# An attention layer's output stage: all five engines in program order, each block's operands joined two blocks ahead

## The chip, the cores and the metric

The kernel runs on one core of a Trainium2 chip. The metric is the device time of one execution in microseconds (us). Engines: PE (TensorE, matmuls; its weight loads are a row of their own, PEld), DVE (VectorE), ACT (ScalarE), POOL (GpSimd), and SP (SyncE), whose queue (SPq) issues all the transfers that this text speaks of. PEclk is the granted TensorE clock, where 1.00 is the 2.4 GHz level and 0.50 the 1.2 GHz level.

## The reference, cut to what matters

Two sequences, a prompt of 1024 tokens and a sample of 2048, go through the same layer. The last lines are what the change is about; the two attentions in front of them are cut to their results.

```python
def hybrid_layer(x, c, w_in, w_out, w_ada, b_ada, ln_g, ln_b, ...):
    shift, scale, gate = jnp.split(jax.nn.silu(c) @ w_ada + b_ada, 3, axis=-1)
    proj = (x * (1.0 + scale[:, None]) + shift[:, None]) @ w_in
    qa, ka, va, ga, qb, kb, vb, gb = jnp.split(proj, SPLIT_OFFSETS, axis=-1)
    oa = window_gqa(qa, ka, va, sink, rel_bias) * jax.nn.silu(ga)
    ob = diff_attention(qb, kb, vb, ...) * jax.nn.silu(gb)     # softmax 1 - lam * softmax 2, then rms_norm
    h = jnp.concatenate([oa, ob], axis=-1) @ w_out             # 1024 x 1024
    return layer_norm(ALPHA * x + gate[:, None] * h, ln_g, ln_b)
```

Every product is wanted at float32's precision. The kernel gets it by splitting each operand into a high part (rounded to the format that PE multiplies at full rate) and a low part (the rest), and multiplying three times: high by high, high by low, low by high.

## The kernel before, in words

The kernel projects, runs the windowed attention (its gated result goes to DRAM as `OA`), and then the differential attention, as a pipeline of *units* (a head and a stretch of queries). A call `slot(n, ...)` does four steps j = 0..3; in each it makes a part of the logits of unit n, the transposes of an earlier unit, and the value products of one still earlier. The unnormalised result of a head goes to DRAM as `OT` (line 876), the row of norm factors as `frow` (line 894); the gate silu(gb) has been in DRAM as `GB` for long.

When the logits of the last unit are issued (unit N-1), six more slots (24 steps) drain the transposes and values. Into each of these steps the kernel puts one step of a generator, `outputs()`, which is printed at the end of this section and does the output product `h` and the layer norm in 24 blocks of 128 tokens: 16 of the sample, then 8 of the prompt. Its parts are:

- `stage` loads w_out; `split_weights(k)` splits 128 rows of it: DVE scales rows 4 to 7 (L989), ACT makes the high half (L990), DVE and POOL the low halves (L991).
- `load_rest(t)` issues five transfers on SP's queue for block t: OT (L999, 256 KB), frow broadcast to all partitions (L1000, 256 KB in SBUF), GB (L1001, 256 KB), OA (L1002, 256 KB), and x (L1004, 512 KB). There are four buffers for the first four (`dat`) and six for x (`xts`).
- `join(t)` makes the left operand of block t: POOL multiplies OT by frow (L1012) and by GB (L1013); then for each of two halves ACT rounds it to the high part (L1016) and POOL subtracts for the low part (L1017). Half 0 is OA and needs only its transfer; half 1 is the product of L1013. There are three buffers for the result (`os_`).
- `output(B)` runs 48 matmuls 128x128 by 128x512 for a block (L1042, L1043, L1044: 2 column halves x 8 k x 3 products) into PSUM (four banks `po`, two to a block), and yields 15 times among them. Behind them stands the layer norm: DVE L1047, L1048, L1051, L1055, L1057; POOL L1058 (the power -1/2); DVE L1080; ACT L1082 twice (from PSUM into x's buffer); POOL L1083 twice (adds the norm's bias); SP L1084 stores 512 KB. The last block has a finer form of its own.

**What sets the order.** In the manual stretch each named engine gets its instructions in the order in which the program writes them. Before, this holds for PE, SP and POOL; ACT's and DVE's order in the tail is made by the framework's scheduler. In the program, `load_rest(t + 3)` comes at step 2 of block t's output and so, on SP, behind the store of block t-1; `join(t + 1)` comes at step 4 of block t's output, and so, on POOL, ahead of the norm of block t (L1058, L1083). Every engine's queue is worked off strictly in its order: an instruction that waits holds up all behind it. A transfer on SP's queue also waits for the one eight transfers before it.

Of the kernel before, what the change touches and what calls it, by code (L numbers as in the profile page):

```python
# [15 lines left out]
PSUM = bass.MemoryType.PSUM  # L16
DRAM = bass.MemoryType.DRAM

PE, SP, POOL = mybir.EngineType.PE, mybir.EngineType.SP, mybir.EngineType.Pool
P = 128  # L20
D = 1024
KC = D // P
# [44 lines left out]
def hybrid_layer(ctx, tc, x_prompt, x_sample, c_prompt, c_sample, w_in, w_out, w_ada, b_ada, ln_g, ln_b,  # L67
# [829 lines left out]
    def slot(n, extra, other=None):  # L897
        for j in range(4):
            if extra:
                fill(extra)  # L900
            if n < N:
                logits(n, j)
                prefetch(n, j)
            for g, piece in values_at.get(n, ()):
                if piece % 4 == j:
                    values(g, piece)
            if 0 <= n - LAG < N:
                transpose(n - LAG, j)
            if j == 1 and n in sums_at:
                square_sum(sums_at[n])  # L910
            if other is not None:
                next(other, None)
# [59 lines left out]
    def stage(ks):  # L972
        for k in ks:
            raws[k] = early_p.tile([P, D], F32, tag="wo", name="raw") if k < 4 else row_halves()
            nc.sync.dma_start(out=raws[k], in_=w_out[k * P:(k + 1) * P, :])
# [7 lines left out]
    def split_weights(k):  # L983
        woH[k], woL[k] = wmem[2 * k](), wmem[2 * k + 1]()
        raw = raws.pop(k)
        for n in range(2):
            ns = slice(n * 512, (n + 1) * 512)
            if k >= 4:
                nc.vector.tensor_scalar(out=raw[:, ns], in0=raw[:, ns], scalar1=wsub, scalar2=None, op0=ALU.mult)  # L989
            nc.scalar.copy(woH[k][:, ns], raw[:, ns])  # L990
            (nc.vector if n else nc.gpsimd).tensor_tensor(  # L991
                out=woL[k][:, ns], in0=raw[:, ns], in1=woH[k][:, ns].bitcast(F32), op=ALU.subtract)

    def load_rest(t):

        s, i = order[t]
        cs = slice(i * P, (i + 1) * P)
        d = dat.next().rearrange("p (n i q) -> p n i q", n=4, i=4)
        nc.sync.dma_start(out=d[:, 1], in_=OT[s][:, :, cs].rearrange("k r t -> r k t"))  # L999
        nc.sync.dma_start(out=d[:, 2], in_=frow[s][:, cs].partition_broadcast(P))  # L1000
        nc.sync.dma_start(out=d[:, 3], in_=GB[s][:, :, cs].rearrange("k r t -> r k t"))  # L1001
        nc.sync.dma_start(out=d[:, 0], in_=OA[s][:, :, cs].rearrange("i r t -> r i t"))  # L1002
        xt = xts.next().bitcast(F32)
        nc.sync.dma_start(out=xt, in_=xs[s][cs, :])  # L1004
        Bs[t] = dict(s=s, i=i, d=d, xt=xt)

    def join(t):

        B = Bs[t]
        d = B["d"]  # L1010
        B["oH"], B["oL"] = [v.rearrange("p (k q) -> p k q", k=KC) for v in os_.next()]
        nc.gpsimd.tensor_tensor(out=d[:, 1], in0=d[:, 1], in1=d[:, 2], op=ALU.mult)  # L1012
        nc.gpsimd.tensor_tensor(out=d[:, 1], in0=d[:, 1], in1=d[:, 3], op=ALU.mult)  # L1013
        for half in range(2):
            hs = slice(half * 4, half * 4 + 4)
            nc.scalar.copy(B["oH"][:, hs, :], d[:, half])  # L1016
            nc.gpsimd.tensor_tensor(out=B["oL"][:, hs, :], in0=d[:, half], in1=B["oH"][:, hs, :].bitcast(F32),  # L1017
                                    op=ALU.subtract)


    def load_gate(s):
        keep[s] = part().bitcast(F32)
        nc.sync.dma_start(out=keep[s], in_=grow[s, :].partition_broadcast(P))

    def load_norm():
        for name, v in (("g", ln_g), ("b", ln_b)):
            keep[name] = part().bitcast(F32)
            nc.sync.dma_start(out=keep[name], in_=v.partition_broadcast(P))
# [58 lines left out]
    NB = len(order)  # L1087
    Bs = {}

    def outputs():  # L1090

        stage((4, 5, 6, 7))
        load_rest(0)
        yield
        for k in range(4):
            split_weights(k)
            yield
        load_gate(1)
        yield
        yield  # L1100
        load_norm()
        yield
        for k in range(4, KC):
            split_weights(k)
            if k == 5:
                join(0)
                load_rest(1)
            yield
        load_rest(2)
        for t in range(NB):  # L1110
            if t == 8:
                load_gate(0)
            for j, _ in enumerate(output(Bs[t], t == NB - 1)):
                if j == 2 and t + 3 < NB:
                    load_rest(t + 3)
                if j == 4 and t + 1 < NB:
                    join(t + 1)
                yield
            del Bs[t]
            yield  # L1120
# [5 lines left out]
    lst.close()  # L1126
    ps_po = pool(st, "ps_po", 4, PSUM)
    other = outputs()
    with tc.manual_schedule(engines={PE, SP, POOL}):
        for n in range(N, max(sums_at) + 1):  # L1130
            slot(n, 0, other)
        for _ in other:
            pass
# [27 lines left out]
```

## Time and profile before

| | us |
|---|---|
| median of 3 runs | 2265.22 (2263.21, 2265.22, 2272.9) |
| the profiled execution, its own time | 2257.25 |
| its span from first to last instruction | 2255.5 |
| what lies around the span | 1.75 |
| PE busy | 2099.9 (93%) |
| DVE, POOL, ACT busy | 1296.5 (57%), 1154.6 (51%), 1037.2 (46%) |

The profiled execution is 7.97 us under the median of the runs. The stretch that the change touches begins at about 1800 us. The views read here are the table of windows (busy time of each engine between two moments), the timeline (every instruction of an engine with its start, its time and, in square brackets, the idle time before it with what ended it), the chain of waits, and the table of waits.

### The profile page before, as it was taken

How to read it: one execution, taken by the hardware profiler on the slowest of the kernel's cores; microseconds unless marked ns; L12 is line 12 of the kernel's file. 1: busy time of each engine (PE TensorE's matmuls, PEld its weight loads, DVE VectorE, ACT ScalarE, POOL GpSimd, SP SyncE). 2: the span in 40 equal slices, each digit the busy share in tenths (PEclk: the TensorE clock that was granted, in tenths of full speed). 3: DMA queues.
4: the chain of work that ended last, by engine and by line, in shares of the span. 5: the costliest groups of instructions: out<-in, count | busy, mean ns of one | idle time of the engine just before them, and what ended most of it. 6: DMA issues, size and time to landing. Idle time of an engine off the chain costs nothing.

```text
span 2255.5 us, 32659 instructions
## 1 busy us (share of the span) xinstructions
PE 2099.9 (93%) x11597; PEld 1793.1 (80%) x11597; DVE 1296.5 (57%) x2538; ACT 1037.2 (46%) x2022; POOL 1154.6 (51%) x836
## 2 busy tenths in 40 slices
PE   7999999999999999999999999999999966777787
PEld 4777988888988788888879999999998854555666
DVE  5343224212246676666459999999998942333444
ACT  5211113111136677666347777777788841111111
POOL 3223223222243343333449888989888952454554
PEclk9999999999999999999999999999999977988999
DMA  8676536445368678775341332314136676454552
GB/s 271 179 261 184 150 126 181 133 118 150 117 186 227 171 190 214 203 192 157 118 151 36 98 63 77 83 39 114 45 91 134 102 99 121 113 137 117 145 150 95
DMA packets 340203, 312.46 MB, mean 139 GB/s; under 512 B 32086, under 2 KB 296950, under 8 KB 339656
## 3 DMA queue, kind: packets, MB, share of 16 engines
q1 hardware_dynamic: 340040, 310.37, 52.1%
q8 instruction: 92, 1.51, 0.4%
q14 instruction: 71, 0.58, 0.2%
HBM read 212.70 MB, written 97.60 MB: 138 GB/s over the span
## 4 chain that ended last, share of the span: by engine, by line
PE 70%; DMA 16%; SPq 4%; DVE 3%; POOL 3%; issue 2%; ACT 1%; ACTq 0%; DVEq 0%; POOLq 0%
PE lg L814 12%; PE pj L186 11%; PE pj L187 11%; PE pj L188 11%; DMA l<-oa 8%; PE tp L852 5%; PE ac L872 3%; PE ac L871 3%; PE ac L870 3%; PE lgA L607 3%; PE tp L643 2%; DMA Q<-qb 2%; PE ac L635 2%; POOL vt L1083 1%; PE ac L634 1%
## 5 line engine op out<-in xcount | busy, mean ns | idle before, releaser
L186 PE MATMUL pj<-uH,wH 128*128 128x512 f32 x1040 | 417.4, 401 | 5.1 <-DVE gg L257 5.1
L188 PE MATMUL pj<-uH,wL 128*128 128x512 f32 x1040 | 407.5, 392 | 0.0
L187 PE MATMUL pj<-uL,wH 128*128 128x512 f32 x1040 | 407.0, 391 | 0.0
L217 POOL TENSOR_TENSOR wL<-wr,wH 128x1024 fp32r<-128x1024 f32 x74 | 181.9, 2460 | 410.7 <-DVE wH L215 368.2
L814 PE MATMUL lg<-kt,Q 128*128 128x512 f32 x1280 | 377.2, 416 | 8.3 <-DMA Q<-qb 6.1
L838 POOL TENSOR_TENSOR l<-l,l 128x1024 f32<-128x1024 f32 x160 | 382.8, 2413 | 0.9
L827 ACT ACTIVATE l<-l,nm 128x2048 f32<-128x2048 f32 (+1 forms) x192 | 331.0, 1724 | 20.9 <-DVE nm L819 20.9
L814 PEld LDWEIGHTS lg<-kt,Q 128*128 128x128 f32 x1280 | 217.3, 190 | 40.8 <-issue 6.6
L819 DVE CUSTOM_DVE_ANT_0 l<-lg,W 128x1024 f32<-128x1024 f32 x192 | 233.2, 1215 | 18.0 <-PE lg L814 17.6
L836 POOL TENSOR_SCALAR l<-l,s 128x1024 f32<-128x1024 f32 x160 | 179.8, 1135 | 116.1 <-DVE s L832 51.2
L854 ACT CAST pth<-tp 128x512 fp32r<-128x512 f32 x320 | 186.2, 583 | 113.6 <-PE tp L852 109.4
L188 PEld LDWEIGHTS pj<-uH,wL 128*128 128x128 f32 x1040 | 195.4, 188 | 42.4
L186 PEld LDWEIGHTS pj<-uH,wH 128*128 128x128 f32 x1040 | 195.9, 188 | 36.8 <-DVE gg L257 5.9
L187 PEld LDWEIGHTS pj<-uL,wH 128*128 128x128 f32 x1040 | 196.2, 189 | 29.9
L855 DVE TENSOR_TENSOR ptl<-tp,pth 128x512 fp32r<-128x512 f32 x320 | 208.7, 684 | 12.1 <-ACT pth L854 10.8
L852 PE MATMUL tp<-ident,l 128*128 128x128 f32 x1280 | 195.9, 276 | 17.1 <-DVE ptl L855 17.0
L872 PE MATMUL ac<-pth,vt 128*128 128x256 f32 x640 | 183.4, 287 | 0.0
L870 PE MATMUL ac<-pth,vt 128*128 128x256 f32 x640 | 183.0, 286 | 0.0
L871 PE MATMUL ac<-ptl,vt 128*128 128x256 f32 x640 | 182.7, 285 | 0.0
L622 POOL TENSOR_SCALAR l<-l,rcA 128x384 f32<-128x384 f32 (+1 forms) x144 | 81.5, 585 | 196.2 <-PE ac L634 85.1
L819 DVE CUSTOM_DVE_ANT_0 l<-lg,W,nm 128x1024 f32<-128x1024 f32 x128 | 164.0, 1281 | 23.7 <-PE lg L814 16.5
L852 PEld LDWEIGHTS tp<-ident,l 128*128 128x128 f32 x1280 | 150.9, 143 | 19.9 <-DVE ptl L855 9.1
(209 smaller groups left out, 4069.8 us busy)
## 6 DMA issues: line engine op xcount, KB each, us to landing
wr<-in_w_in SPq DMA_DIRECT2D x39, 1024.0 KB, 5.4
KAt<-ka SPq DMA_DIRECT2D x40, 384.0 KB, 9.6
QAt<-qa SPq DMA_DIRECT2D x24, 512.0 KB, 4.0
kt<-kb SPq DMA_DIRECT2D x24, 512.0 KB, 9.1
Q<-qb SPq DMA_DIRECT2D x48, 256.0 KB, 3.0
Q<-qb SPq DMA_DIRECT2D x96, 128.0 KB, 4.4
vt<-vb SPq DMA_DIRECT2D x48, 256.0 KB, 5.6
out<-vt SPq DMA_DIRECT2D x20, 512.0 KB, 3.1
```

The costliest lines, as they stand in the source:

```text
L186: nc.tensor.matmul(acc, lhsT=a(k), rhs=b(k), start=(k == 0), stop=False)
L187: nc.tensor.matmul(acc, lhsT=a(k), rhs=bl(k), start=False, stop=False)
L188: nc.tensor.matmul(acc, lhsT=al(k), rhs=b(k), start=False, stop=(k == KC - 1))
L814: nc.tensor.matmul(L[:, c * CH:(c + 1) * CH], lhsT=G["Q"][:, v, m, b * P:(b + 1) * P], rhs=Kt[kt0 + c][:, m, :], start=(v == 0), stop=(v = ...
L819: nc.vector.tensor_tensor_reduce(out=half, in0=L, in1=W[:, off:off + 1024], scale=1.0, scalar=nm[:, m, 0:1] if s and hf else 3e38, op0=ALU ...
L827: nc.scalar.activation(e, e, AF.Exp, bias=nm[:, m, hf:hf + 1], scale=-1.0, accum_out=sums)
L838: nc.gpsimd.tensor_tensor(out=row[:, cs], in0=row[:, cs], in1=rows[n][1][:, cs], op=ALU.add)
L852: nc.tensor.transpose(pt[:, c * P:(c + 1) * P], rows[n][0][:, (j * 4 + c) * P:(j * 4 + c + 1) * P], ident)
L855: nc.vector.tensor_tensor(out=L[:, :, qs], in0=p3, in1=H[:, :, qs].bitcast(F32), op=ALU.subtract)
L870: nc.tensor.matmul(a, lhsT=Vt[kq][:, 0, c, :], rhs=H[:, c, :], start=(kb == 0), stop=False)
L871: nc.tensor.matmul(a, lhsT=Vt[kq][:, 0, c, :], rhs=L[:, c, :], start=False, stop=False)
L872: nc.tensor.matmul(a, lhsT=Vt[kq][:, 1, c, :], rhs=H[:, c, :], start=False, stop=(kb == T - 1))
```

## The change

The set of engines whose order is that of the program becomes all five (`ENGINES`). `join(t + 2)` stands at step 12 of block t's output in place of `join(t + 1)` at step 4; so that this can begin, `join(1)` comes ahead of the first block's output, behind `load_rest(2)`. `load_rest(1)` moves from step k == 5 of the weight splits, where it stood behind `join(0)`, to step k == 4 in front of it. The numbers of instructions stay the same but for a few.

```diff
--- before.py
+++ after.py
@@ -16,7 +16,8 @@
 PSUM = bass.MemoryType.PSUM
 DRAM = bass.MemoryType.DRAM
 
-PE, SP, POOL = mybir.EngineType.PE, mybir.EngineType.SP, mybir.EngineType.Pool
+PE = mybir.EngineType.PE
+ENGINES = {PE, mybir.EngineType.SP, mybir.EngineType.Pool, mybir.EngineType.Activation, mybir.EngineType.DVE}
 P = 128
 D = 1024
 KC = D // P
@@ -1102,19 +1103,21 @@
         yield
         for k in range(4, KC):
             split_weights(k)
+            if k == 4:
+                load_rest(1)
             if k == 5:
                 join(0)
-                load_rest(1)
             yield
         load_rest(2)
+        join(1)
         for t in range(NB):
             if t == 8:
                 load_gate(0)
             for j, _ in enumerate(output(Bs[t], t == NB - 1)):
                 if j == 2 and t + 3 < NB:
                     load_rest(t + 3)
-                if j == 4 and t + 1 < NB:
-                    join(t + 1)
+                if j == 12 and t + 2 < NB:
+                    join(t + 2)
                 yield
             del Bs[t]
             yield
@@ -1126,7 +1129,7 @@
     lst.close()
     ps_po = pool(st, "ps_po", 4, PSUM)
     other = outputs()
-    with tc.manual_schedule(engines={PE, SP, POOL}):
+    with tc.manual_schedule(engines=ENGINES):
         for n in range(N, max(sums_at) + 1):
             slot(n, 0, other)
         for _ in other:
```

The diff doesn't show how instructions are moved on ACT and DVE. First ACT, where the blocks' outputs begin. Lines are one higher after the change (L1016 becomes L1017, L1082 becomes L1083). The `l` buffers of blocks 0 to 3 are `l_18849`, `l_19075`, `l_19134` and `l_19175` before, and `l_18849`, `l_19034`, `l_19134` and `l_19183` after; block 4 takes block 0's again. ACT before, from the last square sums on, with blocks 0 to 2 at the three pairs of L1082:

```order
L887 ACTIVATE ac,ss<-ac 128x128 x2
L1016 CAST Q<-l_19175 128x512
L1082 ACTIVATE vt<-po,ve 128x512 x2
L1016 CAST ptl<-l_19134 128x512
L1016 CAST ptl<-l_18849 128x512
L1082 ACTIVATE vt<-po,ve 128x512 x2
L1016 CAST Q<-l_19175 128x512
L1016 CAST ptl<-l_19075 128x512
L1082 ACTIVATE vt<-po,ve 128x512 x2
```

The same place after, with blocks 0 to 2 at the three pairs of L1083:

```order
L890 ACTIVATE f<-s0g 128x2
L876 COPY osb<-ac 128x256
L1017 CAST ptl<-l_19134 128x512 x2
L1083 ACTIVATE vt<-po,ve 128x512 x2
L1017 CAST Q<-l_19183 128x512 x2
L1083 ACTIVATE vt<-po,ve 128x512 x2
L1017 CAST ptl<-l_18849 128x512 x2
L1083 ACTIVATE vt<-po,ve 128x512 x2
```

Before, the first half of block 3 stands ahead of block 0's norm pair, and the first half of block t+3 ahead of block t's from there on; after, both halves of block t+2 stand there and nothing of block t+3.

Second, DVE at the end of the logits (L819 takes a row's maximum, L855 makes the low part of a transpose for which PE waits, L989 scales w_out's rows). Before:

```order
L855 TENSOR_TENSOR ptl<-tp,pth 128x4x128
L819 ISA l_18704,nm<-lg,W 128x1024
L819 ISA nm 128x1
L989 TENSOR_SCALAR l_18843<-l_18843,wsub 128x512 x2
L829 RECIPROCAL s_18703<-s_18703 128x1
L855 TENSOR_TENSOR ptl<-tp,pth 128x4x128
L891 TENSOR_SCALAR f<-ss,f 128x1
L989 TENSOR_SCALAR l_18843<-l_18843,wsub 128x512
L819 ISA l_18769,nm<-lg,W 128x1024
```

DVE after, at the same place:

```order
L856 TENSOR_TENSOR ptl<-tp,pth 128x4x128
L820 ISA l_18704,nm<-lg,W 128x1024
L820 ISA nm 128x1
L830 RECIPROCAL s_18703<-s_18703 128x1
L856 TENSOR_TENSOR ptl<-tp,pth 128x4x128
L892 TENSOR_SCALAR f<-ss,f 128x1
L820 ISA l_18769,nm<-lg,W 128x1024
```

The scaling of w_out's rows (L989, now L990) no longer stands between the maxima and the transposes; it comes at steps 8 to 11 of the drain, where the program writes it.

## Rows read from the trace of the kernel before

**Rows 1.** Windows of 50 us: window, length, PE, PEld, DVE, ACT, POOL busy, PEclk, DMA share, GB/s.
```profile
1850.00:1900.00 50.00, 27.73 (x128) 22.98 (x128) 9.97 (x20) 4.31 (x17) 11.10 (x11) 0.80 0.72 129
...
2150.00:2200.00 50.00, 41.54 (x176) 32.49 (x175) 22.11 (x38) 7.84 (x13) 31.18 (x28) 1.00 0.51 148
```
**Rows 2.** Timeline of SP: stores of blocks 0, 12 and 19 (start, length).
```profile
1904.25 0.34 SPq L1084 DMA_DIRECT2D out<-vt  x1
...
2110.22 0.35 SPq L1084 DMA_DIRECT2D out<-vt  x1
...
2206.99 0.35 SPq L1084 DMA_DIRECT2D out<-vt  x1
```
**Rows 3.** Chain of waits, 2002 to 2024: start, us, what held the end.
```profile
1993.18 10.32 DMA l<-oa
...
2004.12 0.69 ACT vt L1082
...
2006.13 1.29 POOL vt L1083
```
**Rows 4.** Timeline of ACT, then of POOL, same block.
```profile
2003.60 0.62 ACT L1016 CAST Q<-l 128x512 fp32r<-128x512 f32 x1 [9.77 <-DMA l<-oa]
...
2008.72 1.26 POOL L1013 TENSOR_TENSOR l<-l 128x512 f32<-128x512 f32 x1
2009.94 2.51 POOL L1017 TENSOR_TENSOR pth<-l,ptl 128x512 fp32r<-128x512 f32 x2
2012.40 0.56 POOL L1058 TENSOR_TENSOR ve<-ve,mhalf 128x1 f32<-128x1 f32 x1
```
**Rows 5.** Waits, 1905 to 2250: waiting line <- releaser: total us, times, longest.
```profile
POOL vt L1083 <- ACT vt L1082: 131.8, 19, 9.9
...
PE po L1042 <- ACT vt L1082: 0.7, 1, 0.7
```
**Rows 6.** Timeline of PE in a prompt block; the first two rows lie 46 starts apart.
```profile
2155.73 0.39 PE L1042 MATMUL po<-kt,ptl 128*128 128x512 f32 x1
...
2166.39 0.40 PE L1043 MATMUL po<-kt,Q 128*128 128x512 f32 x1
2169.15 0.51 PE L1044 MATMUL po<-kt,Q 128*128 128x512 f32 x1 [2.36 <-POOL Q L1017]
```
**Rows 7.** Windows (columns as in rows 1): a sample block, a prompt block, the drain.
```profile
2007.50:2011.00 3.50, 0.00 (x0) 0.00 (x0) 3.29 (x7) 0.62 (x1) 3.42 (x3) 1.00 0.77 231
2011.00:2015.50 4.50, 4.24 (x12) 3.35 (x13) 0.04 (x1) 0.00 (x0) 1.96 (x3) 0.62 0.26 39
2015.50:2020.50 5.00, 5.00 (x23) 4.08 (x22) 2.10 (x3) 0.35 (x1) 0.00 (x0) 1.00 0.70 219
2020.50:2024.40 3.90, 3.70 (x16) 2.65 (x15) 0.56 (x1) 1.44 (x3) 2.96 (x3) 1.00 0.01 4
2138.50:2141.50 3.00, 0.92 (x4) 0.39 (x3) 2.30 (x4) 0.62 (x1) 2.92 (x3) 0.98 0.95 285
...
2144.00:2148.50 4.50, 4.50 (x19) 3.62 (x18) 0.00 (x0) 0.84 (x2) 0.00 (x0) 0.91 0.79 242
...
1832.50:1840.00 7.50, 5.40 (x40) 5.23 (x40) 5.52 (x9) 4.97 (x13) 6.15 (x6) 0.89 0.00 0
```
**Rows 8.** Timelines of the drain and the end, by engine: PE, ACT, DVE.
```profile
1815.06 1.09 PE L852 MATMUL tp<-ident,l 128*128 128x128 f32 x4 [4.62 <-DVE ptl L855]
1829.14 1.11 PE L852 MATMUL tp<-ident,l 128*128 128x128 f32 x4 [7.51 <-DVE ptl L855]
...
1883.09 0.62 ACT L1016 CAST ptl<-l 128x512 fp32r<-128x512 f32 x1 [8.36 <-DMA l<-oa]
...
1900.42 0.62 ACT L1016 CAST Q<-l 128x512 fp32r<-128x512 f32 x1 [14.03 <-DMA l<-oa]
...
1892.00 0.70 DVE L1047 TENSOR_TENSOR po<-po,pth 128x512 f32<-128x512 f32 x1 [4.76 <-PE po L1044]
...
2247.07 0.43 DVE L1047 TENSOR_TENSOR po<-po,pth 128x256 f32<-128x256 f32 x1 [1.50 <-PE po L1044]
```

## The prediction

> **What bounds the kernel now.** I read the windows of 50 us first, since the share of the whole span hides the last stretch. From 1850 to 1900 PE works for 27.7 us of 50 at a granted clock of 0.80; from 2150 to 2200, where it is at full clock, it works 41.5 [rows 1]. So in the last 400 us something other than PE sets the time. The stores of the blocks give the pace: block 0's starts at 1904.25, block 12's at 2110.22, block 19's at 2206.99 [rows 2]; that is 205.97 / 12 = 17.16 us a block, and then 96.77 / 7 = 13.82. The first twelve gaps have a sample block's load behind the store, the others a prompt block's.
>
> What PE itself wants is less. At full clock 46 starts take 2166.39 - 2155.73 = 10.66 us, 0.232 us each, so a block of 48 takes 11.1 us, and then PE stands for 2.36 us until L1017 has made the next block's operand [rows 6].
>
> The chain of waits says what the 17.16 us are. One lap reads: block t+3's OA lands after 10.32 us, ACT's first L1082 takes 0.69 us, POOL's last L1083 1.29 us, then the store and the next load are issued and the next OA is waited for [rows 3]. The link that need not be there is on ACT: L1016 stands idle for 9.77 us for block t+3's OA, and the norm of block t (L1082), long ready, stands behind it [rows 4]. POOL's L1083 waits 131.8 us in 19 blocks for that L1082 [rows 5], 6.9 us each. SP's store waits for L1083, and the load of block t+4 stands behind the store. So a load can't be issued until the load before it has landed: one load at a time. The windows show it as seen from the transfers: from 2007.5 the DMA engines are busy with 0.77, 0.26 and 0.70 of their time until 2020.5, then 0.01 until the next store [rows 7].
>
> **The change part by part.** *ACT's order and the join two blocks ahead* go together. L1016 ahead of block t's L1082 is now that of block t+2, both halves, and not the first half of block t+3. Block t+2's load was issued behind the store of block t-2. So the lap closes over two blocks. It gets longer: besides the 17.16 us, L1082 now stands behind the second half's L1016, POOL's norm behind both L1017 (2.51) and L1058 (0.56) [rows 4], 3.1 us if nothing covers them. That is 20.2 us for two blocks, 10.1 a block: less than PE's 11.1. POOL's own work in a block, six operations of 1.26 or so and one of 0.56 [rows 4], is 8.1 us, also less. No operation is added; the join's work on POOL is the same as before, and is now hidden behind the matmuls of the block in between. What is late next is either PE, at 11.1 us, or the transfers.
>
> *The transfers* must then do a store and five loads in each block's time. Before they were alone, so two bounds can be read. Alone, from the store at 2007.5 to the last load at 2020.5, a sample block takes up to 13.0 us; I take 12.5, as the OA that is waited for lands a little ahead of that end. Summed by share, the work is 0.77 x 3.5 + 0.26 x 4.5 + 0.70 x 5.0 = 7.4 us [rows 7], the least that a packed stream could take. A prompt block takes 10.0 us alone, 2138.5 to 2148.5 [rows 7]. For the sample I take 12.5, the upper bound, since in the middle 4.5 us only 39 GB/s move [rows 7]: a slow transfer on few engines, which the next block's copy of the same transfer can queue behind. For the prompt 10.0 is under PE's 11.1, so PE sets the pace there. At a pace of 12.5 PE's gaps are 1.4 us; gaps of 2.36 us left the clock at 1.00 in 2150 to 2200 [rows 1, 6], so I take 11.1 us at full clock for a block.
>
> [...]
>
> *DVE's order at the end of the logits.* L989 leaves the place between the maxima and the transposes. There it waited for w_out's rows, and PE's transposes waited for DVE's L855 behind it: 4.62 and 7.51 us [rows 8], 12.1 us in all. The DMA engines idled 7.5 us at 1832.5 to 1840 [rows 7], because what is issued next on SP hangs on the same drain. I take these 12.1 us as gained by all that follows, so block 3's OA, landed at 1900.42 before [rows 8], lands at 1888.3. Against it: the eight casts of L990 for k = 4 to 7 now stand on ACT in the drain's steps 8 to 11. They aren't shown here; the nearest row is L1016 with the same 128x512 at 0.62 [rows 8], so 8 x 0.62 = 5.0 us if none is hidden, and 0 if all are. I take 0, because 27.7 of 50 us of PE in that stretch [rows 1] leave ACT room, and keep 5.0 for the range. `join(1)` ahead of block 0 costs POOL 5.0 us (four operations of 1.26) in the same stretch, with the same cover; if that is gone, 5.0 more.
>
> *`load_rest(1)` one step earlier* puts five transfers ahead of one frow store (L894) on SP. Its price lies between nothing and one wait like that of 8.36 us for OA in the same stretch [rows 8]; I take nothing, since block 0 doesn't need it.
>
> **The sum.** From block 3's OA: 12 sample loads at 12.5 = 150.0; the second gate row, 512 KB at 231 GB/s, an estimate of 2.3; the first prompt load 10.0; its join 1.26 + 0.62 + 1.26 = 3.1; eight blocks of PE at 11.1 = 88.8; from the last matmul to the end 2255.5 - 2247.07 = 8.4 [rows 8]. Together 262.6, on 1888.3: a span of 2150.9. With 1.75 around it the profiled execution would be 2152.7, against 2257.25 before: 104.6 us less. The profiled execution of before lay 7.97 under the median, so I add 7.97 and forecast **2161 us**.
>
> **The rivals.** *PE paces all blocks*: the transfers pack to under 11.1. Block 0's last product came just before 1892.0 [rows 8], less 12.1 is 1879.9; 23 x 11.1 = 255.3 and 8.4 give 2143.6, so 2153 us. For it speaks the summed 7.4; against it the slow middle part.
>
> *The drain gains nothing*: another wait (the w_out split late on ACT, the frow stores) takes the place of DVE's. Then 12.1 us stay: 2173. Against it: the two stalls are put to DVE by name [rows 8].
>
> *The transfers slow each other down*: between block 2's and block 3's OA, with loads back to back, lie 1900.42 - 1883.09 = 17.3 us [rows 8], more than 12.5. Halfway to it, at 15.5 for the sample and 13.0 for the prompt, 12 x 3.0 + 3.0 + 7 x 1.9 = 52 us come on top: 2213.
>
> *Slower than before*: the whole of that. The broadcast of frow queues behind itself in each block as at block 3, 17.3 us, and the store of 512 KB adds some 2 at 231 GB/s, so 19.3 for a sample block and, 2.5 less, 16.8 for a prompt block. 1888.3 + 12 x 19.3 + 2.3 + 8 x 16.8 + 3.1 + 11.1 + 8.4 = 2279, so 2289 us. It decides from about 18.1 us on a sample block. Against it: in that stretch SP also waited for w_out's and the norm rows' loads, and the same load with nothing beside it took 10.32 [rows 3].
>
> *It doesn't do what it says*: buffers hold the loads. The Trainium skill (Perfetto Trace Analysis, Optimization Strategy) says that a gap which repeats on the engine that should be busy can mean too few buffers; the gaps of PE here do repeat. In this trace PE waits for an accumulator to come free (L1042 for L1082) 0.7 us in all [rows 5], and the four buffers of a load allow the fourth block ahead, so I give it little: the pace stays, and the time is within 0.5% of 2265.
>
> **How the numbers follow.** Forecast 0.50; PE alone 0.20; drain without gain 0.10; transfers in each other's way 0.10; no effect 0.05; slower 0.05. The range reaches from the PE-paced case with some of its own spread (2153 less 13, the 7.97 and 5.0 that I may have added wrongly) to the case of slowed transfers (2213); that leaves out the last two and a little of each side. Half a percent (11 us) is about what a measurement of this kernel can tell from no change: faster 0.90, same 0.05, slower 0.05.
>
> **What would show it.** Right: ACT's L1082 follows PE's last product of its block within some 4 us, POOL's wait for it is near nothing; stores are 12.5 us apart in the sample, 11.1 in the prompt; the clock is 1.00 from about 1900 on; L855 in the drain waits for nothing of w_out. It would be wrong if ACT's L1016 still waits for OA in every block with gaps over 13 us: then the transfers are the bound at another price than mine. If stores come every 11.1 us from the start, PE sets them.

## The result, and the profile after

The changed kernel takes **2143.55 us** (median of 4 runs, 2140.66 to 2150.52) against 2264.22 us for the kernel before in the same comparison: a ratio of 0.9465, with a 95% interval of 0.943 to 0.950. The forecast was 2161 us with a range of 2140 to 2213. The profiled execution took 2145.12 us with a span of 2143.3. The profiled execution of the kernel before lay 8 us under its median, so the spans differ by less than the medians do.

Where the 112.2 us of span went can be read from two moments, DVE's first operation on the last columns of block 0 and of block 23 (L1047 before, L1048 after). Before they lie at 1892.00 and 2247.07 [rows 8]. The same rows of after, with block 7 and block 19 between them, from the timeline of DVE:

```profile
1877.12 0.70 DVE L1048 TENSOR_TENSOR po<-po,pth 128x512 f32<-128x512 f32 x1 [3.39 <-PE po L1045]
...
1957.20 0.70 DVE L1048 TENSOR_TENSOR po<-po,pth 128x512 f32<-128x512 f32 x1 [3.40 <-PE po L1045]
...
2090.59 0.70 DVE L1048 TENSOR_TENSOR po<-po,pth 128x512 f32<-128x512 f32 x1 [3.40 <-PE po L1045]
...
2135.21 0.43 DVE L1048 TENSOR_TENSOR po<-po,pth 128x256 f32<-128x256 f32 x1 [1.50 <-PE po L1045]
```

| stretch | before, us | after, us | gain |
|---|---|---|---|
| start to block 0's product | 1892.0 | 1877.1 | 14.9 |
| the 23 blocks after it | 355.1 | 258.1 | 97.0 |
| from there to the end | 8.4 | 8.1 | 0.3 |

So most of the gain lies in the blocks. From block 7 to block 19 they come every (2090.59 - 1957.20) / 12 = 11.12 us, with no difference between sample and prompt. The windows of 50 us, to be read against [rows 1], say that PE has become the bound (window, length, PE, PEld, DVE, ACT, POOL busy, PEclk, DMA share, GB/s):

```profile
1850.00:1900.00 50.00, 41.42 (x187) 34.33 (x188) 19.24 (x35) 10.96 (x31) 25.38 (x23) 0.90 0.84 135
1900.00:1950.00 50.00, 48.09 (x209) 38.68 (x208) 26.69 (x47) 10.05 (x16) 33.77 (x29) 1.00 0.73 195
1950.00:2000.00 50.00, 50.00 (x217) 40.52 (x216) 25.65 (x44) 12.56 (x20) 38.10 (x34) 1.00 0.71 198
```

PE is busy for all 50 us at a clock of 1.00, and the DMA engines move 198 GB/s, where they moved 231, 39, 219 and 4 by turns within one block before [rows 7]. The table of waits shows the link that is gone (waiting line, releaser, total us, times, longest):

```profile
ACT ptl L1017 <- DMA l<-oa: 62.2, 13, 13.3
...
POOL vt L1084 <- ACT vt L1083: 15.8, 19, 0.9
```

POOL waited 131.8 us in 19 blocks for ACT's norm [rows 5]; now 15.8, which is 0.8 each. ACT still waits for OA, but on another block's behalf and at no one's cost, as its timeline in the sample shows:

```profile
1993.99 0.62 ACT L1017 CAST Q<-l 128x512 fp32r<-128x512 f32 x1 [4.76 <-DMA l<-oa]
1995.06 0.62 ACT L1017 CAST Q<-l 128x512 fp32r<-128x512 f32 x1 [0.45 <-POOL l L1014]
1998.08 1.27 ACT L1083 ACTIVATE vt<-po,ve 128x512 f32<-128x512 f32 x2 [2.40 <-POOL ve L1059]
```

The norm (L1083) stands behind a wait of 4.76 us here too. But it is a wait for block t+2's load, which was issued behind the store of block t-2 and not of block t-1; PE has a whole block of work in the meantime.

### The profile page after: what moved, and what is told of

It reads as the page before. It is cut to its first block, busy times and chain, and to the rows that moved or that the text cites. A ratio compares the mean times of both kernels' runs of the same rounds, so it can differ in the third digit from the quotient of the medians.

```text
span 2143.3 us, 32639 instructions
## 1 busy us (share of the span) xinstructions
PE 2074.8 (97%) x11597; PEld 1778.4 (83%) x11597; DVE 1297.6 (61%) x2538; ACT 1038.9 (48%) x2022; POOL 1156.6 (54%) x836
## 4 chain that ended last, share of the span: by engine, by line
PE 84%; DMA 9%; DVE 2%; SPq 1%; POOL 1%; issue 1%; ACT 1%; DVEq 0%; POOLq 0%; ACTq 0%
PE lg L815 13%; PE pj L187 11%; PE pj L188 11%; PE pj L189 11%; PE tp L853 6%; PE po L1043 4%; PE po L1044 3%; PE po L1045 3%; PE ac L873 3%; PE ac L872 3%; PE ac L871 3%; PE lgA L608 3%; PE tp L644 2%; DMA Q<-qb 2%; PE ac L636 2%; DMA l<-frow 1%
## 5 line engine op out<-in xcount | busy, mean ns | idle before, releaser
L855 ACT CAST pth<-tp 128x512 fp32r<-128x512 f32 x320 | 186.1, 582 | 123.8 <-PE tp L853 118.7
L856 DVE TENSOR_TENSOR ptl<-tp,pth 128x512 fp32r<-128x512 f32 x320 | 209.2, 685 | 18.0 <-ACT pth L855 16.2
L820 DVE CUSTOM_DVE_ANT_0 l<-lg,W,nm 128x1024 f32<-128x1024 f32 x128 | 164.1, 1282 | 24.1 <-PE lg L815 17.1
L613 ACT ACTIVATE l<-l,nmA 128x385 f32<-128x385 f32 (+1 forms) x192 | 115.4, 601 | 87.8 <-DVE nmA L610 72.1
```

The source lines that it names most:

```text
L820: nc.vector.tensor_tensor_reduce(out=half, in0=L, in1=W[:, off:off + 1024], scale=1.0, scalar=nm[:, m, 0:1] if s and hf else 3e38, op0=ALU ...
L856: nc.vector.tensor_tensor(out=L[:, :, qs], in0=p3, in1=H[:, :, qs].bitcast(F32), op=ALU.subtract)
```

## The experiments

Theory A: in the kernel before, one place in ACT's order, the first half of block t+3 ahead of the norm of block t, closes a lap over one block's load. Theory B: the join two blocks ahead is what helps, by taking POOL's work out of PE's way. Each ratio is taken against the kernel before, run beside that kernel.

| kernel | median, us | block 0's product | 23 blocks |
|---|---|---|---|
| before | 2264 | 1892.0 | 355.1 |
| the change | 2143.55 | 1877.1 | 258.1 |
| order_only | 2150.31 | 1878.2 | 259.5 |
| join_only | 2253.73 | 1886.4 | 352.0 |
| act_join | 2160.86 | 1893.3 | 257.3 |
| dve_join | 2251.48 | 1889.8 | 354.9 |
| hoist_back | 2242.13 | 1878.7 | 353.8 |

The last two columns are from the profiled execution of each, read as above. A difference of a few us to the row of before isn't to be relied on, since that execution ran 8 us under its median.

### order_only: the order without the earlier join

```diff
-                if j == 12 and t + 2 < NB:
-                    join(t + 2)
+                if j == 4 and t + 1 < NB:
+                    join(t + 1)
```

(`join(1)` ahead of block 0 goes as well, and `load_rest(1)` stands behind `join(0)` again.)

> All five engines in program order, the joins and loads where they were before (block t+1 joined at step 4 of block t's output). Theory A (the lap is closed by ACT's order: block t+3's first half ahead of block t's norm; the join's place is of no account): stores 11.2 us apart, 2145 us, 8 either way. Theory B (the join two blocks ahead is what takes POOL's work off PE's way): PE still waits some 2.4 us a block for L1018, 23 x 2.4 = 55 us more than the change, 2199 us.

Measured: 2150.31 us, ratio 0.9503 (0.9483 to 0.9523). Its window of the sample blocks:

```profile
1950.00:2000.00 50.00, 50.00 (x218) 40.40 (x217) 27.27 (x47) 11.47 (x18) 35.77 (x31) 1.00 0.79 198
```

PE is busy throughout, just as with the early join. Theory B's 2.4 us a block aren't there. The earlier join is worth what lies between the two medians, 6.8 us, or nothing: the two intervals overlap.

### join_only: the earlier join without the order

```diff
-ENGINES = {PE, mybir.EngineType.SP, mybir.EngineType.Pool, mybir.EngineType.Activation, mybir.EngineType.DVE}
+ENGINES = {PE, mybir.EngineType.SP, mybir.EngineType.Pool}
```

> The join and load moves of the change, with only PE, SP and POOL in program order; ACT and DVE stay with the scheduler, which again puts block t+3's first half ahead of block t's norm on ACT. Theory A: stores 17.2 and then 13.8 us apart as before, 2265 us (2255 to 2272). Theory B: most of the gain, 2165 us.

Measured: 2253.73 us, ratio 0.9955 (0.9938 to 0.9972), so 0.45% of the change's 5.35%. Theory A had said 2255 to 2272, which is missed by 1.3 us. Its ACT timeline reads as before:

```profile
1982.48 0.62 ACT L1017 CAST ptl<-l 128x512 fp32r<-128x512 f32 x1 [10.06 <-DMA l<-oa]
1983.01 1.26 ACT L1083 ACTIVATE ptl<-po,ve 128x512 f32<-128x512 f32 x2
...
1999.66 0.62 ACT L1017 CAST Q<-l 128x512 fp32r<-128x512 f32 x1 [10.07 <-DMA l<-oa]
2000.19 1.26 ACT L1083 ACTIVATE vt<-po,ve 128x512 f32<-128x512 f32 x2
```

The wait of 10 us for OA is straight ahead of the norm, and the norms are 17.2 us apart. Theory B is out.

### act_join and dve_join: one engine's order each

```diff
-ENGINES = {PE, ..., mybir.EngineType.Activation, mybir.EngineType.DVE}
+ENGINES = {PE, ..., mybir.EngineType.Activation}      (act_join)
+ENGINES = {PE, ..., mybir.EngineType.DVE}             (dve_join)
```

> The change with ACT, but not DVE, in program order. Theory A: stores 11.2 us apart, and the drain of the logits as before, since DVE's scaling of w_out stands among the maxima again: 12 to 15 us more than the change, 2157 us. If DVE's order counts in the blocks too: over 2200. If DVE's order is of no account in the drain: 2144.

> The change with DVE, but not ACT, in program order. Theory A: the lap stays at 17.2 and 13.8 us, and the drain gains 12 to 15 us: 2251 us. If DVE's order mattered in the blocks: under 2200.

Measured: 2160.86 us (ratio 0.9545, 0.953 to 0.956) and 2251.48 us (0.9948, 0.993 to 0.9966). With the join moved, ACT's order without DVE's gives all of the blocks' gain (257.3 us, where join_only has 352.0). DVE's order without ACT's gives none there. In the drain, with ACT's order, DVE's brings block 0's product forward by 1893.3 - 1877.1 = 16.2 us. Of these 3.6 lie ahead of the drain, since the last logits end at 1822.4 in act_join and at 1818.8 in the change. Two rows of act_join's timeline (PE, then DVE) show how DVE's place costs time:

```profile
1830.24 1.11 PE L853 MATMUL tp<-ident,l 128*128 128x128 f32 x4 [7.15 <-DVE ptl L856]
...
1828.71 0.88 DVE L990 TENSOR_SCALAR l<-l,wsub 128x512 f32<-128x512 f32 x2 [9.06 <-DMA l<-in_w_out]
```

DVE waits 9.06 us for w_out's rows, PE 7.15 us for DVE. In the changed kernel the longest such wait of PE after 1820 is this one:

```profile
1836.24 0.66 PE L853 MATMUL tp<-ident,l 128*128 128x128 f32 x4 [1.50 <-DVE ptl L856]
```

Without ACT's order DVE's brings block 0's product no earlier: it comes at 1886.4 in join_only and at 1889.8 in dve_join, where PE still waits 15.0 us for DVE in the drain (17.4 in join_only, 5.6 in the change). So the drain's gain isn't a sum of two independent parts. dve_join's total came as expected, but not by the drain's 12 to 15 us that it was to come from. act_join takes 17.3 us more than the change, where 12 to 15 were expected.

### hoist_back: one place put back

```diff
+    def first_half(t):
+        B = Bs[t]
+        B["early"] = True
+        B["oH"], B["oL"] = [v.rearrange("p (k q) -> p k q", k=KC) for v in os_.next()]
+        nc.scalar.copy(B["oH"][:, 0:4, :], B["d"][:, 0])
...
+        hook()
         mv = sA_p.tile([P, 2], F32, tag="mv", name="mv")
...
-            for j, _ in enumerate(output(Bs[t], t == NB - 1)):
+            for j, _ in enumerate(output(Bs[t], t == NB - 1, lambda: first_half(t + 3) if t + 3 < NB else None)):
```

(`join` then skips what `first_half` has done.)

> The changed kernel, all five engines in its program order and the joins two blocks ahead, with one thing put back: ACT rounds the first half of block t+3 ahead of block t's norm (21 casts moved by one place). Theory A (this one place closes the one-block lap): stores 17.2 us apart in the sample and 13.8 in the prompt again, 94 us more than the change, 2238 us (2225 to 2255). If the gain came from the order of the engines in general or from the earlier join: under 2165 us.

Measured: 2242.13 us, ratio to the kernel before 0.9893 (0.9877 to 0.991). With 21 casts moved by one place, 98.6 us of the change's 120.7 are gone. Stores of blocks 0, 12 and 19 in its SP timeline, to be read with [rows 2], one of its waits, and its ACT timeline:

```profile
1892.67 0.34 SPq L1094 DMA_DIRECT2D out<-vt  x1
...
2100.93 0.35 SPq L1094 DMA_DIRECT2D out<-vt  x1
...
2198.47 0.35 SPq L1094 DMA_DIRECT2D out<-vt  x1
```
```profile
POOL vt L1093 <- ACT vt L1092: 134.2, 19, 11.4
```
```profile
1992.29 0.62 ACT L1028 CAST Q<-l 128x512 fp32r<-128x512 f32 x1 [9.72 <-DMA l<-oa]
1992.82 1.26 ACT L1092 ACTIVATE vt<-po,ve 128x512 f32<-128x512 f32 x2
```

The stores are (2100.93 - 1892.67) / 12 = 17.36 and (2198.47 - 2100.93) / 7 = 13.93 us apart (17.16 and 13.82 before), and POOL's wait for ACT is back at 134.2 us. This is theory A, shown by one change in one place. What it keeps is the drain's: of the 14.9 us by which its span (2240.6) is under that of before, 13.3 are gained by block 0's product, at 1878.7.

### lean, lean_nofrow, lean_order: what the transfers need when PE isn't the bound

The third product (L1045) is left out, so PE needs 7.4 us a block at full clock. The windows of lean from 1900 to 2050 show a clock of 0.86 to 0.93 and PE busy for 35 to 40 of 50 us, so PE still isn't the bound. lean_nofrow also leaves out the broadcast of frow, and multiplies by the gate twice in its place.

```diff
-                nc.tensor.matmul(a, lhsT=oH[:, k, :], rhs=woL[k][:, ns], start=False, stop=False)
-                nc.tensor.matmul(a, lhsT=oL[:, k, :], rhs=woH[k][:, ns], start=False, stop=(k == KC - 1))
+                nc.tensor.matmul(a, lhsT=oH[:, k, :], rhs=woL[k][:, ns], start=False, stop=(k == KC - 1))
```
```diff
-        nc.sync.dma_start(out=d[:, 2], in_=frow[s][:, cs].partition_broadcast(P))
...
-        nc.gpsimd.tensor_tensor(out=d[:, 1], in0=d[:, 1], in1=d[:, 2], op=ALU.mult)
+        nc.gpsimd.tensor_tensor(out=d[:, 1], in0=d[:, 1], in1=d[:, 3], op=ALU.mult)
```

> The changed kernel with the third product (L1045, low by high) left out of every block, so PE needs 32 x 0.232 = 7.4 us a block and stops being the bound; everything else is as it was. What then sets the pace of the stores: if the transfers need 12.5 us a block as forecast, the pace can't fall and stays at or over 11.1; if the two-block lap sets it, 20.2 / 2 = 10.1 us, some 2118 us in all; if the transfers pack and POOL sets it, 8.1 to 8.5 us, some 2075 us.

> The kernel above, and also without the broadcast load of frow (L1001 goes; L1013 multiplies by the gate GB in its place), which is the transfer behind the slow stretch of 39 GB/s. If the transfers set the pace of the kernel above, it falls here by 2 us a block or more; if the lap or POOL sets it, by under 1 us.

> The joins one block ahead, all five engines in program order, and the third product (L1045, low by high) left out of every block: a lap of three blocks' loads in place of two, with PE at 7.4 us a block. The changed kernel without that product stored every 11.0 us in the sample. If the two-block lap, lengthened by slower loads, set those 11.0: they fall towards the 9.0 of the prompt, some 2097 us. If the transfers' own work sets them: 11.0 stays within 0.3, 2118 to 2126 us.

Measured in one execution each: 2120.07, 2083.96 and 2118.89 us. Stores of blocks 3 and 11 of lean, of the same blocks of lean_order, and two that lie eight blocks apart in lean_nofrow:

```profile
1921.16 0.35 SPq L1084 DMA_DIRECT2D out<-vt  x1
...
2009.31 0.35 SPq L1084 DMA_DIRECT2D out<-ptl  x1
```
```profile
1927.81 0.38 SPq L1084 DMA_DIRECT2D out<-vt  x1
...
2013.07 0.38 SPq L1084 DMA_DIRECT2D out<-ptl  x1
```
```profile
1907.15 0.35 SPq L1083 DMA_DIRECT2D out<-vt  x1
...
1978.93 0.35 SPq L1083 DMA_DIRECT2D out<-ptl  x1
```

In the sample that is 88.15 / 8 = 11.02 us a block for lean, 85.26 / 8 = 10.66 for lean_order, and 71.78 / 8 = 8.97 for lean_nofrow. One of the eight gaps also holds the 512 KB of the second gate row. In lean_nofrow POOL is busy for 45.54 of 50 us, so POOL sets its pace:

```profile
1950.00:2000.00 50.00, 43.64 (x184) 33.90 (x183) 33.06 (x58) 13.42 (x22) 45.54 (x40) 1.00 0.67 209
```

lean's pace is set by the lap over two blocks. Its chain of waits (start, us, what) runs from a store through the load of frow, POOL's join and the norm to the next store but one, lap after lap; this is the lap from block 6's store to block 8's:

```profile
1954.07 0.35 SPq L1084
...
1954.95 11.46 DMA l<-frow
...
1966.54 1.29 POOL l L1013
...
1969.14 2.54 POOL pth L1018 x2
...
1972.22 0.70 ACT vt L1082
...
1972.99 2.55 POOL vt L1083 x2
...
1975.55 0.35 SPq L1084
```

That is 21.48 us for two blocks, and the three laps beside it take up to 22.05, where I had forecast 20.2. Beside the other transfers frow takes 11.46 us from the end of its issue to its landing. I had expected 10.1 us a block and some 2118 us if this lap sets the pace, and 2120 came. In lean_order, whose lap has one block more, SP's stores hardly wait for a norm any more. The largest of SP's waits between the two stores shown, for lean and then for lean_order (waiting line, releaser, total us, times, longest):

```profile
SPq L1084 <- POOL vt L1083: 11.4, 7, 2.4
```
```profile
SPq L1084 <- POOL vt L1083: 0.8, 1, 0.8
```

Of lean_order's chain between these stores 84% are SP's issues and the landings of frow and OA. So a sample block's transfers take some 10.7 us back to back, and not 12.5. lean's pace is only 0.36 us a block over that, which is why lean_order gains so little. Without the broadcast of frow the pace falls to POOL's 8.97, so the broadcast costs the stream 10.66 - 8.97 = 1.69 us a block or more. The fall of 2.05 us from lean to lean_nofrow doesn't tell the transfers from the lap, though my expectation took it so: the load of frow is a part of lean's lap, too.

### join1_late, load1_early, load12_early, sp_logits: four tries to be faster still

In the changed kernel PE stands 8.30 us behind ACT's square sums, which stand behind `join(1)`'s wait for OA (PE, then ACT):

```profile
1863.83 0.58 PE L871 MATMUL ac<-pth,vt 128*128 128x256 f32 x1 [8.30 <-ACT ac L888]
...
1861.42 0.62 ACT L1017 CAST ptl<-l 128x512 fp32r<-128x512 f32 x1 [7.93 <-DMA l<-oa]
```

```diff
         load_rest(2)
-        join(1)
         for t in range(NB):
...
+                if t == 0 and j == 2:
+                    join(1)
```

> The changed kernel with join(1) moved from ahead of block 0's output to step 2 of it, so that ACT's square sums (L888) no longer stand behind the join's L1017 that waits for block 1's OA. If that is what holds PE for 8.30 us at 1863.8 in the changed kernel: 5 to 8 us less, 2137 us. If block 0 is held by its own loads or the next blocks take the gain back: 2143 us, no change.

Measured: 2145.17 us, 0.9469 (0.9454 to 0.9485), no change. Block 0's product comes 2.9 us earlier, at 1874.2, and the 23 blocks take 2.3 us longer, so the second expectation came true.

load1_early also brings `load_rest(1)` ahead of `load_gate(1)` and `load_rest(2)` to k == 6; load12_early brings `load_rest(2)` right behind `load_norm()`:

```diff
+        load_rest(1)
         load_gate(1)
...
         load_norm()
+        load_rest(2)
```

> The changed kernel with join(1) at step 2 of block 0's output, load_rest(1) ahead of the gate row and the norm rows on SP, and load_rest(2) at step k == 6 of the weight splits. If the start of the blocks is held by block 1's load, which stands on SP behind those rows: block 0 and block 1 follow without a gap, 8 us less than the change, 2136 us. If the row buffers or the last frow stores hold these loads on SP: no gain, or the stores behind them come late, 2143 to 2155 us.

> As load1_early, with load_rest(2) right behind the norm rows, some 20 us earlier still. By the first theory the third block's load is out of the way too: 2133 us. By the second it holds SP's queue longer: 2145 to 2160 us.

Measured: 2145.88 (0.9472 to 0.9506) and 2144.79 us (0.9458 to 0.9504): no gain. In load1_early another wait has come in the place of the old one (PE, then ACT):

```profile
1872.51 0.69 PE L886 MATMUL ac<-ident,osb 128*128 128x128 f32 x2 [9.08 <-ACT osb L876]
...
1872.09 0.37 ACT L876 COPY osb<-ac 128x256 f32<-128x256 f32 x1 [11.91 <-DMA ot<-osb]
```

ACT now waits for a store of `osb`; that the earlier loads beside it made this store slow is likely, but wasn't tried. The blocks run without a gap from there (255.9 us, 11.13 each), but block 0 comes 2.3 us later than in the change, at 1879.4.

```diff
-        for n in range(EARLY, N):
+        for n in range(EARLY, N - 4):
             slot(n, 0)
+    with tc.manual_schedule(engines={PE, mybir.EngineType.SP}):
+        for n in range(N - 4, N):
+            slot(n, 0)
```

> The changed kernel with SP, beside PE, in program order in the last four slots of the logits too. In the changed kernel the last logits end 11 us later than before, behind waits for the queries' loads, which stand on SP behind a frow store. If that order is the cause: the 11 us come back, 2133 us. If the values' loads, which the program writes late, now come too late: slower than the change, over 2150 us.

Measured: 2148.19 us, 0.949 (0.947 to 0.9511), which is 4.6 over the change, with overlapping intervals. The last logits end at 1818.8 as in the change (1807.5 before). SP's order in these four slots isn't what delays them. The delay stays open: it lies ahead of the changed stretch, where the scheduler plans SP and POOL anew for each kernel, and in the other kernels the logits end between 1809 and 1822.

## Why the prediction was right, and where it was off

**What bounded the kernel**: right, and shown by hoist_back. The lap of 17.16 us through ACT's idle L1016 was the bound of the blocks, and it was closed by that one place in ACT's order.

**The lap over two blocks, 10.1 us, under PE's 11.1**: right that it lies under PE's, but by less than I thought. Where PE doesn't bound, in lean, a lap takes 21.48 to 22.05 us, 10.7 to 11.0 a block, and frow, which it waits for, takes 11.46 us to land. In the changed kernel PE is busy 50.0 of 50 us. The clock is 1.00 from 1900 on, as said.

**PE's 11.1 us a block**: right; 11.12 from block 7 to block 19.

**The drain's 12.1 us**: right in size, but only in part by the cause that I named. Block 3's OA was forecast for 1888.3, and ACT takes it at 1889.27:

```profile
1889.27 1.14 ACT L1017 CAST Q<-l 128x512 fp32r<-128x512 f32 x2 [7.50 <-DMA l<-oa]
```

Block 0's product came 14.9 us earlier. Not foreseen was that the last logits end 11.3 us later (1818.8 against 1807.5), so the drain from there to block 0's product is 26.2 us shorter. PE's two largest waits in the drain, from the last logits to 1880, before and then after (waiting line, releaser, total us, times, longest):

```profile
PE ac L885 <- ACT osb L875: 18.3, 1, 18.3
PE tp L852 <- DVE ptl L855: 16.0, 5, 7.5
```
```profile
PE ac L871 <- ACT ac L888: 8.3, 1, 8.3
PE tp L853 <- DVE ptl L856: 5.6, 5, 1.5
```

The waits for DVE, which I had priced, give 10.4 of the 26.2 us. The longest wait for ACT is 10.0 us shorter, which I hadn't foreseen; the rest wasn't taken apart. That these gains less the later logits come out near 12.1 is in part luck. And `join(1)`, which I had priced as work of POOL, costs PE 8.30 us by ACT's wait for block 1's OA: the same mechanism as in the blocks before, an operand's wait ahead of other work.

**The transfers' 12.5 us**: wrong, and the term of the sum that was mis-sized. It was read from a load that stood alone, and I took that upper bound of 7.4 to 13.0. Back to back a sample block takes 10.7 us (lean_order), just under PE's 11.1, so PE paced the blocks: from block 0's product to block 23's it is busy but for one gap of 1.91 us. That was my first rival: its span was 2143.6 us, the measured one is 2143.3. That they agree so closely is luck, since block 0's product came 2.8 us earlier than the rival has it, and the blocks took 2.8 us longer. I gave it 0.20, and the forecast 0.50.

**The offset of 7.97 us**: wrong. The profiled execution of before was 7.97 us under the median; that of after is 1.57 over it. Of the 17.1 us by which my sum (2160.7 before rounding) is too high, 7.6 are the span (2150.9 against 2143.3) and 9.5 this offset. It is the spread of single runs, and I should have kept it in the range alone.

**The slower rival, 19.3 us a block by the queueing broadcasts**: no. It decided from 18.1; the packed stream needs 10.7. That the broadcast is a slow transfer was right (1.69 us a block or more), but it doesn't queue behind itself for 17 us.

**Too few buffers**: no. With the same buffers PE is busy but for that one gap. The Trainium skill (Perfetto Trace Analysis, Optimization Strategy) says that a gap which repeats on the engine that should be busy can mean too few buffers. Here the gaps repeated in every block, and hoist_back shows that an instruction's place in ACT's queue made them.

**The signs I named**: POOL's wait near nothing, the clock, and L856 in the drain came as said. The stores 12.5 us apart in the sample didn't come; the blocks are 11.1 apart in sample and prompt alike, as in the last sign. The norm was to follow PE's last product within 4 us; it follows later (block 10's by some 7.5 us, 1990.55 to 1998.08), since it stands behind block t+2's join, and PE waits for a norm only in the one gap of 1.91 us.

## What to carry to other kernels

When a block-wise pipeline runs slower than each of its engines, follow the chain of waits around one lap and ask at each in-order engine what stands ahead of the instruction that is late: an operand of a later block, hoisted ahead of it, can tie the store of this block to the load of the next but two. The remedy is the order, and a test of it is to put that one instruction back. And the time of a block's load that stands alone isn't its price in a stream: here 12.5 us were forecast from it and 10.7 measured. When a rival bound lies between the two ends of such a range (11.1 between 7.4 and 13.0), the two cases should get like chances.

## What the runs showed of the hardware that was not expected

A block's transfers, alone up to 13.0 us from the store to the last load [rows 7], took 10.7 us in a stream (lean_order). Of these the broadcast of 256 KB cost 1.69 us or more, though it is one eighth of the 2048 KB that a block moves. And PE's clock stood at 1.00 in the windows of lean_nofrow with PE busy for 43.64 of 50 us (6.4 us of gaps over 5.6 blocks, 1.1 a block), while in hoist_back it was 0.83 in the same window with PE busy for 39.60 (10.4 us over 2.9 blocks, 3.6 a block). What of this difference lowered the clock wasn't tried:

```profile
1950.00:2000.00 50.00, 39.60 (x140) 30.82 (x139) 17.14 (x30) 7.21 (x12) 22.74 (x21) 0.83 0.45 125
```
